# A one-core decoder layer: which queue writes the class-ordered attention values to DRAM, and when they are read back

## The chip, the cores and the metric

The kernel runs on one core of one Trainium2 chip. The metric is the device time of one execution in microseconds (us), the median over repeated runs. The engines are named as the profile names them: PE (TensorE, the matmuls), PEld (its weight loads), DVE (VectorE), ACT (ScalarE), POOL (GpSimd) and SP (SyncE). ACT, POOL and SP each issue DMAs from their own instruction stream, in program order: an instruction that waits holds up everything behind it on the same engine. PEq, ACTq, POOLq and SPq are the instruction queues of these engines.

## The reference

One layer of a decoder on x of 512 tokens by 1024 columns, float32. What matters here is the middle of it, the dilated attention; around it stand a gated linear attention, a merge, an MLP and a second gate:

```python
h = rmsnorm(x, ln1)
hq, hk, hv, hr, ha, hatt, hgate = split(h @ w_in)      # 9744 columns in all
o_gla = gla_mixer(hq, hk, hv, log_a)                    # gated linear attention, chunks of 64
hatt = hatt.reshape(B, S, 3 groups, 3 (q, k, v), 4 heads, 128)
for g, (win, dil) in enumerate(((128, 1), (512, 4), (2048, 16))):
    # a query sees keys t, t-dil, t-2*dil, ...: keys and values are gathered by stride
    o_g, lse_g = dilated_attention(q_g, k_g, v_g, bias_g, dil, win // dil)
wts = softmax(stack(lses), axis=0)                      # over the three groups
o_att = sum(wts * stack(outs))
mix = (sigmoid(g_gla) * (o_gla' @ w_o_gla) + sigmoid(g_att) * (o_att @ w_o_attn)) @ w_out
x = x + mix
x = x + relu(rmsnorm(x) @ w_mlp1)**2 @ w_mlp2
x = x + sigmoid(rmsnorm(x) @ w_pg) * (p @ w_pp)
return rmsnorm(x)
```

For the groups with stride 4 and 16 the kernel keeps the tokens ordered by class, token number modulo 4. Their values v1 and v2 (512 tokens by 512 columns each) leave the projection in natural order, so they are written to DRAM and read back with a stride of four rows: tile c of the result holds the tokens with t mod 4 = c.

## The kernel before

**The products.** All large products are done as one block level of a seven-product scheme (Strassen's, in Winograd's form), in float32 split into two parts `hi` and `lo`, with three matmuls for each pair. For each quarter of a weight matrix, called an operand, there are seven weight combinations, used in this order: A11, S1, A22, S2, A12, S4, S3. `strassen` (L338) runs them for most projections and `wide` (L384) for v1 and v2 together (the name is "v12"), as left-hand side 128 tokens by 512 columns. The projection after "v12" is "v0", the values of the first group, and the one after that "gq".

**How weights arrive.** `fetch` (L269) walks one list of operands, a few ahead of the matmul that needs them. For each it does four things, one operand apart: `prepare` (L238) issues the load on SP (L235), and, for the sum S1, a second load on POOL that adds to the tile in flight (L243); `sums` (L247) builds S2 and S4 on DVE (L255, L261) and, at S2, issues the accumulating load on POOL that turns the tile of A11 into S3 (L258); then ACT rounds `hi` (L281) and DVE subtracts `lo` (L276). There are six raw tiles `w`, five `hi` and four `lo`.

**The order of the work.** The program is written out in order by hand; nothing reorders it later but the hardware's own waits. Between pieces of eight or fewer matmuls `step` (L213) runs one entry of the list `later` (evacuations of PSUM and what follows them), and, after every so many matmul columns (`pace`), one step of a generator in `side` (work such as scores and softmax, up to the next `yield`); up to two generators in `side` take turns.

**The place of the change.** `values_cls` (L760) calls `wide`, whose `finish` is run from `later` once for each of the eight blocks of 128 tokens by 512 columns. `whole` (L740) makes the block: for six blocks a DVE add of PSUM to a partial sum (L422), for the last two an ACT copy out of PSUM (L744). POOL then writes the block to `v_dram` (L767). After the fourth block of a matrix, POOL reads the four tiles of that matrix back (L772). The last two blocks are finished during the first matmuls of "v0". Behind them on POOL come, in program order, the accumulating load L258 for operand S3 of "v0" and two small DMAs of the generator `weights` (L850): `k_dram` (L879) and `cc` (L880), which bring the softmax weights of the strided groups into natural order. `pv` (L890) uses `cc` first on DVE (L896), and the tiles v1 and v2 on PE (L932, L933), both during "gq".

Of the kernel before, what the change touches and what calls it, by code (L numbers as in the profile page):

```python
# [19 lines left out]
P = 128  # L20
# [161 lines left out]
def block_kernel(ctx, tc, xT, ws, pT, wts, wha, wa2, vec, lnf, rel, onehot, ident_d, mask_d, out):  # L182
    nc = tc.nc
    V, S, TE, SY, GP = nc.vector, nc.scalar, nc.tensor, nc.sync, nc.gpsimd
# [11 lines left out]
    def u32(name="u"):  # L196
        return ar.tile([P, T], F32, tag="u", name=name)
# [4 lines left out]
    def mmt():  # L202
        return mm.tile([P, T], F32, tag="mm", name="mmt")

    def smt():
        return sm.tile([P, T], F32, tag="sm", name="smt")


    side, later = [], []
# [78 lines left out]
    def weight(name, ahead=NW - 3):  # L288
        fetch(OPERAND[name] + ahead)
        return ready[name]  # L290

    def run(mms, n=PIECE, shared=False):
        for i in range(0, len(mms), n):
            for o, l, r, a, b in mms[i:i + n]:
                TE.matmul(o, lhsT=l, rhs=r, start=a, stop=b, skip_group_check=shared)  # L295
            step(n * r.shape[-1])
# [87 lines left out]
    def wide(name, xo, finish):  # L384


        bank, sums = {}, {}

        def begin(m, t, n, b):
            def go():  # L390
                sums[m, t, n] = u32()
                S.activation(sums[m, t, n], bank[b][n], AF.Copy, scale=-1.0 if m else 1.0)
            return go

        def end(m, t, n, b):
            return lambda: finish(m, t, n, sums.get((m, t, n)), bank[b][n])

        for i, (op, xname, b) in enumerate(WIDE):
            fresh = b not in bank
            if fresh:  # L400
                bank[b] = [smt() if b == "b" else mmt() for _ in range(2)]
            for pr in range(4):
                wh, wl = weight(f"{name}.{op}.{pr // 2}")
                xh, xl = xo(xname, pr)
                r = slice((pr % 2) * 512, (pr % 2 + 1) * 512)
                mms = []
                for n in range(2):
                    c = slice(n * P, (n + 1) * P)
                    for k, (l, w) in enumerate(((xh, wh), (xl, wh), (xh, wl))):
                        mms.append((bank[b][n], l[:, c], w[:, r], fresh and not pr and not k, pr == 3 and k == 2))  # L410
                run(mms, 3, shared=True)
            if i in WBEGIN:
                (m, t), b = WBEGIN[i]
                later[0:0] = [begin(m, t, n, b) for n in range(2)]
            if i in WEND:
                (m, t), b = WEND[i]
                later.extend(end(m, t, n, b) for n in range(2))
# [322 lines left out]
    def whole(m, s, ps):  # L740

        if s is None:
            s = u32()
            S.activation(s, ps, AF.Copy, scale=-1.0 if m else 1.0)  # L744
        else:
            add(m, s, s, ps)
        return s
# [12 lines left out]
    def values_cls(name):  # L760

        v_dram = [dr.tile([T, 512], F32, name=f"v{m}_dram") for m in range(2)]
        res, left = [[], []], [4, 4]

        def finish(m, t, n, s, ps):
            s, r = whole(m, s, ps), (2 * t + n) * P
            GP.dma_start(v_dram[m][r:r + P, :], s)  # L767
            left[m] -= 1
            if not left[m]:
                for c in range(4):  # L770
                    v = u32()
                    GP.dma_start(v, v_dram[m].rearrange("(m c) f -> c m f", c=4)[c])  # L772
                    res[m].append(v)

        wide(name, xs_op, finish)
        return res

    def softmax(ps, n0, bias, nm, sums, col, prob):
# [377 lines left out]
    side.append(scores12())  # L1156
    pace[0] = 3072
    v1, v2 = values_cls("v12")
    pace[0] = 2048
    side.append(weights())  # L1160
# [428 lines left out]
    def put(tt, c):  # L1589
        n = c.stop - c.start  # L1590
        o = u32()
        V.scalar_tensor_tensor(out=o[:, 0:n], in0=x2t[4 + tt][:, c], scalar=fr[:, tt:tt + 1], in1=lnb[1][:, c],
                               op0=OP.mult, op1=OP.mult)
        SY.dma_start(out[tt * P:(tt + 1) * P, 512 + c.start:512 + c.stop], o[:, 0:n])
# [112 lines left out]
```

## Time and profile before

| | |
|---|---|
| median time | 965.9 us |
| lowest time | 965.85 us |
| the profiled execution | 968.71 us |
| its span | 966.9 us |
| mean granted PE clock of the profiled execution | 0.994 |
| PE busy | 954.6 us, 99% |
| DVE busy | 740.6 us, 77% |
| ACT busy | 543.9 us, 56% |
| POOL busy | 101.5 us, 10% |
| moved by DMA | 140.97 MB, mean 146 GB/s |

The span runs from the first to the last instruction of the profiled execution; the execution's own time is 1.8 us longer. In a timeline row stand start and duration, engine, line, operation, output and inputs, how many, and in brackets how long the engine sat idle before it and what released it. A row of waits has the total, how often, and the longest. In a table by stretch come the length, busy time with the number of instructions for PE, PEld, DVE, ACT and POOL, then the granted PE clock (1.00 is full), the busy share of the 16 DMA engines and the GB/s that they moved.

### The profile page before, as it was taken

How to read it: one execution, taken by the hardware profiler on the slowest of the kernel's cores; microseconds unless marked ns; L12 is line 12 of the kernel's file. 1: busy time of each engine (PE TensorE's matmuls, PEld its weight loads, DVE VectorE, ACT ScalarE, POOL GpSimd, SP SyncE). 2: the span in 40 equal slices, each digit the busy share in tenths (PEclk: the TensorE clock that was granted, in tenths of full speed). 3: DMA queues.
4: the chain of work that ended last, by engine and by line, in shares of the span. 5: the costliest groups of instructions: out<-in, count | busy, mean ns of one | idle time of the engine just before them, and what ended most of it. 6: DMA issues, size and time to landing. Idle time of an engine off the chain costs nothing.

```text
span 966.9 us, 16069 instructions
## 1 busy us (share of the span) xinstructions
PE 954.6 (99%) x6398; PEld 880.4 (91%) x6398; DVE 740.6 (77%) x1062; ACT 543.9 (56%) x886; POOL 101.5 (10%) x143
## 2 busy tenths in 40 slices
PE   9999999989999999999999999999999999999997
PEld 8789998889998899999988889999998998998886
DVE  7698879746789669988765788777767999787754
ACT  7357547435575569776632346555655664354633
POOL 0140010220100012023001000010000000000000
PEclk9999999989999999999999999999999999999999
DMA  9374373965636554546526437556564374553102
GB/s 325 116 233 119 117 175 72 300 197 132 147 94 199 170 154 117 146 132 196 153 88 196 131 71 182 162 134 173 155 173 109 110 176 107 134 194 109 44 0 88
DMA packets 42923, 140.97 MB, mean 146 GB/s; under 512 B 6435, under 2 KB 7023, under 8 KB 42848
## 3 DMA queue, kind: packets, MB, share of 16 engines
q1 hardware_dynamic: 28224, 95.37, 29.3%
q0 software_dynamic: 12096, 42.17, 21.5%
q10 hardware_dynamic: 2528, 2.41, 0.7%
q8 instruction: 50, 0.82, 0.3%
q14 instruction: 25, 0.20, 0.1%
HBM read 133.60 MB, written 8.17 MB: 147 GB/s over the span
## 4 chain that ended last, share of the span: by engine, by line
PE 92%; DVE 3%; ACT 2%; DMA 1%; issue 1%; POOL 0%; POOLq 0%; DVEq 0%; ACTq 0%
PE mmt L295 77%; PE smt L295 6%; PE mmt L552 2%; PE smt L976 1%; DMA w<-in_wts_dram 1%; DVE lo L276 1%; PE smt L916 1%; PE smt L839 1%; DVE u L422 0%; PE smt L524 0%; ACT hi L281 0%; PE smt L933 0%; PE smt L809 0%; PE smt L932 0%; PE smt L922 0%
## 5 line engine op out<-in xcount | busy, mean ns | idle before, releaser
L295 PE MATMUL mmt<-ur,hi 128*128 128x256 f32 (+1 forms) x3120 | 635.8, 301 | 0.0
L295 PEld LDWEIGHTS mmt<-ur,hi 128*128 128x128 f32 x3120 | 500.7, 188 | 21.8
L295 PE MATMUL mmt<-ur,lo 128*128 128x256 f32 (+1 forms) x1560 | 470.7, 302 | 0.0
L276 DVE TENSOR_TENSOR lo<-w,hi 128x1024 fp32r<-128x1024 f32 x250 | 303.2, 1219 | 57.3 <-PE mmt L295 27.7
L281 ACT ACTIVATE hi<-w 128x1024 fp32r<-128x1024 f32 x250 | 260.9, 1054 | 110.6 <-PE mmt L295 25.9
L295 PEld LDWEIGHTS mmt<-ur,lo 128*128 128x128 f32 x1560 | 294.0, 188 | 10.9
L295 PE MATMUL mmt<-hi,ur 128*128 128x512 f32 (+3 forms) x480 | 134.7, 366 | 4.3 <-ACT u L369 4.3
L429 ACT ACTIVATE ur<-u 128x512 fp32r<-128x512 f32 x130 | 77.2, 624 | 98.1 <-DVE u L1241 30.8
L295 PEld LDWEIGHTS mmt<-hi,ur 128*128 128x128 f32 x480 | 87.0, 193 | 17.0 <-ACT u L369 4.5
L422 DVE TENSOR_TENSOR u<-u,mmt 128x512 f32<-128x512 f32 (+1 forms) x116 | 73.1, 655 | 38.1 <-PE mmt L295 37.9
L437 DVE TENSOR_TENSOR ur<-u,ur 128x512 fp32r<-128x512 f32 x129 | 84.8, 686 | 16.5 <-ACT ur L429 16.1
L295 PE MATMUL mmt<-lo,ur 128*128 128x512 f32 (+3 forms) x240 | 87.2, 363 | 0.0
L369 ACT ACTIVATE u<-mmt 128x512 f32<-128x512 f32 x88 | 52.3, 594 | 52.8 <-PE mmt L295 52.4
L243 POOL DMA_DIRECT2D w<-in_wts_dram x32 | 28.8, 923 | 309.6 <-DMA w<-in_wts_dram 102.8
L258 POOL DMA_DIRECT2D w<-in_wts_dram x24 | 21.2, 884 | 332.6 <-DVE w L255 239.8
L295 PEld LDWEIGHTS mmt<-lo,ur 128*128 128x128 f32 x240 | 46.3, 193 | 6.6
L295 PE MATMUL smt<-ur,hi 128*128 128x512 f32 x160 | 50.4, 393 | 0.1
L295 PEld LDWEIGHTS smt<-ur,hi 128*128 128x128 f32 x160 | 29.7, 188 | 8.1 <-PE smt L649 0.8
L295 PE MATMUL smt<-ur,lo 128*128 128x512 f32 x80 | 31.2, 390 | 0.0
L255 DVE TENSOR_TENSOR w<-w 128x1024 f32<-128x1024 f32 x24 | 29.4, 1225 | 0.8
L261 DVE TENSOR_TENSOR w<-w 128x1024 f32<-128x1024 f32 x24 | 29.4, 1225 | 0.8
L462 ACT ACTIVATE u<-u 128x512 f32<-128x512 f32 x24 | 14.9, 622 | 16.7 <-DVE u L1322 16.7
(213 smaller groups left out, 767.8 us busy)
## 6 DMA issues: line engine op xcount, KB each, us to landing
w<-in_wts_dram SPq DMA_DIRECT2D x170, 512.0 KB, 4.4
w<-in_wts_dram POOLq DMA_DIRECT2D x56, 512.0 KB, 5.7
u<-in_xT_dram SPq DMA_DIRECT2D x8, 256.0 KB, 5.0
u<-in_ws_dram SPq DMA_DIRECT2D x8, 256.0 KB, 5.2
v_dram<-u POOLq DMA_DIRECT2D x8, 256.0 KB, 9.1
u<-v_dram POOLq DMA_DIRECT2D x8, 256.0 KB, 6.1
y_dram<-u ACTq DMA_DIRECT2D x8, 256.0 KB, 3.6
u<-y_dram POOLq DMA_DIRECT2D x8, 256.0 KB, 5.9
```

What stands on the lines that cost most here:

```text
L243: GP.dma_start(w, wts[UNIT[b]], accum_op=OP.add)
L255: V.tensor_tensor(w, w, raw[f"{q}.A11"], op=OP.add)
L258: GP.dma_start(w, wts[UNIT[f"{q}.A21"]], accum_op=OP.add)
L261: V.tensor_tensor(w, w, raw[f"{q}.A12"], op=OP.add)
L276: V.tensor_tensor(lo, w, hi.bitcast(F32), op=OP.subtract)
L281: S.activation(hi, w, AF.Copy)
L295: TE.matmul(o, lhsT=l, rhs=r, start=a, stop=b, skip_group_check=shared)
L369: S.activation(sums[c], bank[b], AF.Copy, scale=-scale if c[0] else scale)
L422: V.tensor_tensor(out, s, ps, op=OP.subtract if m else OP.add)
L429: S.activation(hi, x, AF.Copy)
L437: V.tensor_tensor(lo, x, hi.bitcast(F32), op=OP.subtract)
L552: TE.matmul(q0ps[i], lhsT=(hi, hi, lo)[j][:, c], rhs=(xh, xl, xh)[j], start=not k and not j, stop=k == KC - 1 and j == 2)
```

## The change

The write of a block to `v_dram` is issued by ACT instead of POOL, and not in `finish` itself but in an entry that `finish` puts at the end of `later`, so some steps after the block is made. The read-back becomes a generator `back` in `side`. It waits, yielding, until all eight writes are issued, yields once more, and issues the four reads of the first matrix in one step and the four of the second in its next. The counter of writes left is one for both matrices.

```diff
     def values_cls(name):
 
         v_dram = [dr.tile([T, 512], F32, name=f"v{m}_dram") for m in range(2)]
-        res, left = [[], []], [4, 4]
+        res, left = [[], []], [8]
 
         def finish(m, t, n, s, ps):
             s, r = whole(m, s, ps), (2 * t + n) * P
-            GP.dma_start(v_dram[m][r:r + P, :], s)
-            left[m] -= 1
-            if not left[m]:
+
+            def put():
+                S.dma_start(v_dram[m][r:r + P, :], s)
+                left[0] -= 1
+            later.append(put)
+
+        def back():
+            while left[0]:
+                yield
+            yield
+            for m in range(2):
                 for c in range(4):
                     v = u32()
                     GP.dma_start(v, v_dram[m].rearrange("(m c) f -> c m f", c=4)[c])
                     res[m].append(v)
+                yield
 
         wide(name, xs_op, finish)
+        side.append(back())
         return res
```

The change adds ten lines, so lines of the kernel before from L773 on have numbers higher by ten in the kernel after; the write is L769 there and the read L780.

On POOL, from the last weight loads of "v12" to the first of "gk", before; `v_dram` is one of the two DRAM arrays, `u` a tile in SBUF:

```order
L243 DMA w<-in_wts_dram 128x1024 x5
L767 DMA v_dram<-u 128x512 x4
L243 DMA w<-in_wts_dram 128x1024
L767 DMA v_dram<-u 128x512 x2
L772 DMA u<-v_dram 128x512 x4
L258 DMA w<-in_wts_dram 128x1024
L767 DMA v_dram<-u 128x512 x2
L772 DMA u<-v_dram 128x512 x4
L879 DMA k_dram<-u 16x128
L880 DMA cc<-k_dram 128x4x4
L243 DMA w<-in_wts_dram 128x1024
L258 DMA w<-in_wts_dram 128x1024 x2
```

The same stretch on POOL after the change:

```order
L243 DMA w<-in_wts_dram 128x1024 x6
L258 DMA w<-in_wts_dram 128x1024
L780 DMA u<-v_dram 128x512 x8
L889 DMA k_dram<-u 16x128
L890 DMA cc<-k_dram 128x4x4
L243 DMA w<-in_wts_dram 128x1024
L258 DMA w<-in_wts_dram 128x1024 x2
```

The load for S3 of "v0" (the single L258) stood behind six writes and four reads and now has none of them ahead; all eight reads stand together behind it, and ahead of the two small DMAs.

On ACT, over the end of "v12" and the first operand of "v0", before; `e` with a number is a small tile of `weights`:

```order
L825 DMA u<-s_dram 32x128
L281 ACTIVATE hi<-w 128x1024 x8
L744 ACTIVATE u<-mmt 128x512
L861 ACTIVATE e_1987<-e_1987 128x16
L862 ACTIVATE e_1988<-e_1988 128x16
L744 ACTIVATE u<-mmt 128x512
L281 ACTIVATE hi<-w 128x1024
L369 ACTIVATE u<-mmt 128x512
```

The same stretch on ACT after the change:

```order
L835 DMA u<-s_dram 32x128
L281 ACTIVATE hi<-w 128x1024 x2
L769 DMA v_dram<-u 128x512 x2
L281 ACTIVATE hi<-w 128x1024 x2
L769 DMA v_dram<-u 128x512 x2
L281 ACTIVATE hi<-w 128x1024 x2
L769 DMA v_dram<-u 128x512 x2
L281 ACTIVATE hi<-w 128x1024 x2
L744 ACTIVATE u<-mmt 128x512 x2
L871 ACTIVATE e_1988<-e_1988 128x16
L872 ACTIVATE e_1989<-e_1989 128x16
L769 DMA v_dram<-u 128x512
```

Three pairs of writes now stand between the roundings of weights; of the last pair one stands here and the other behind the first evacuation of "v0" (L369), ahead of the rounding after it.

On DVE, over the same operands of "v0", before; `cn` and `dn` are small tiles of `weights`:

```order
L869 TENSOR_TENSOR cn_355<-e_1987,dn 128x16
L870 TENSOR_TENSOR cn_1991<-e_1988,dn 128x16
L276 TENSOR_TENSOR lo<-w,hi 128x1024
L261 TENSOR_TENSOR w<-w 128x1024
L877 COPY u<-smt 16x128
L276 TENSOR_TENSOR lo<-w,hi 128x1024 x4
```

And after:

```order
L879 TENSOR_TENSOR cn_355<-e_1988,dn 128x16
L880 TENSOR_TENSOR cn_1992<-e_1989,dn 128x16
L276 TENSOR_TENSOR lo<-w,hi 128x1024 x2
L887 COPY u<-smt 16x128
L276 TENSOR_TENSOR lo<-w,hi 128x1024 x2
```

Since `back` and `weights` take turns in `side`, the steps of `weights` come later: the copy that `k_dram` is written from now stands two operands further on, during the fifth operand of "v0" instead of the third.

## The prediction

> **What bounds the kernel now.** I start with the page's busy times and its chain, then ask which waits stopped PE.
>
> ```profile
> PE 954.6 (99%) x6398; PEld 880.4 (91%) x6398; DVE 740.6 (77%) x1062; ACT 543.9 (56%) x886; POOL 101.5 (10%) x143
> PE 92%; DVE 3%; ACT 2%; DMA 1%; issue 1%; POOL 0%; POOLq 0%; DVEq 0%; ACTq 0%
> ```
>
> PE is busy for 99% of the span and carries 92% of the chain. No change to DMA queues can therefore win more than what PE loses by waiting. The waits of PE over the whole span, most of all first:
>
> ```profile
> PE mmt L295 <- ACT u L369: 4.3, 1, 4.3
> PE smt L524 <- POOL ones L519: 1.0, 1, 1.0
> PE smt L976 <- DVE ur L1039: 0.2, 1, 0.2
> PE smt L916 <- ACT u L908: 0.2, 1, 0.2
> ```
>
> There is one wait of 4.3 us, one at the start that the change can't reach, and two of 0.2 us. The chain of the whole span shows where the long one lies and what is behind it:
>
> ```profile
> 194.86 11.38 DMA w<-in_wts_dram
> 207.87 0.94 ACT hi L281
> 209.35 8.62 PE mmt L295 x48
> ...
> 407.32 5.69 PE mmt L295 x48
> ```
>
> PE comes back at 209.35 us, and the chain before that is a weight load on its way for 11.38 us. ACT's rows name the load's customer, POOL's rows its issue:
>
> ```profile
> 206.32 1.06 ACT L281 ACTIVATE hi<-w 128x1024 fp32r<-128x1024 f32 x1 [11.98 <-DMA w<-in_wts_dram]
> 208.71 0.59 ACT L369 ACTIVATE u<-mmt 128x512 f32<-128x512 f32 x1
> 182.75 1.22 POOL L767 DMA_DIRECT2D v_dram<-u  x2 [0.72 <-DVE u L422]
> 192.75 2.13 POOL L772 DMA_DIRECT2D u<-v_dram  x4 [8.77 <-DMA v_dram<-u]
> 194.86 0.94 POOL L258 DMA_DIRECT2D w<-in_wts_dram  x1
> 195.42 1.48 POOL L767 DMA_DIRECT2D v_dram<-u  x2
> 208.43 2.14 POOL L772 DMA_DIRECT2D u<-v_dram  x4 [11.53 <-issue]
> 184.30 1.23 DVE L255 TENSOR_TENSOR w<-w 128x1024 f32<-128x1024 f32 x1
> ```
>
> ACT stood still for 11.98 us until operand S3 of "v0" had landed. POOL issued that load (L258) at 194.86. The data allowed it from 185.53 on, when DVE's L255 had read the raw tile (184.30 + 1.23). In between POOL sat for 8.77 us in front of the first read of `v_dram`, until the writes issued at 182.75 had landed, and then issued four reads. So POOL's program order made the load 194.86 - 185.53 = 9.3 us late. That the DMA engines were not the reason is in the stretches:
>
> ```profile
> 188.00:190.00 2.00, 2.00 (x19) 2.00 (x18) 1.90 (x7) 1.45 (x3) 0.00 (x0) 1.00 1.01 371
> 192.00:194.00 2.00, 2.00 (x19) 1.98 (x18) 1.21 (x2) 0.82 (x2) 1.25 (x3) 1.00 0.02 8
> 202.00:204.00 2.00, 2.00 (x20) 2.00 (x19) 0.00 (x0) 0.00 (x0) 0.00 (x0) 1.00 1.01 268
> 210.00:212.00 2.00, 2.00 (x11) 2.00 (x11) 1.97 (x4) 1.19 (x2) 1.07 (x3) 0.50 0.86 199
> ```
>
> Between 192 and 194 us the DMA engines are 2% busy while the load waits for its turn on POOL. By 202 us they are full again with the load, the reads and the writes together.
>
> **What the wait costs PE.** There are two terms. The idle time itself is in this row:
>
> ```profile
> 209.35 0.58 PE L295 MATMUL mmt<-hi,ur 128*128 128x256 f32 x1 [4.26 <-ACT u L369]
> ```
>
> The first term is 4.26 us. The second is the clock: the last stretch above has a granted clock of 0.50, and the 48 matmuls from 209.35 on take 8.62 us, while 48 of the same shape at 407.32 take 5.69. That is 2.93 us more. Together 7.19 us.
>
> **The change, part by part.**
>
> *The load for S3 goes ahead of the reads.* POOL's rows ahead of it are only weight loads now, so L258 is issued when L255 is done, at about 185.6. What does it take to land? The nearest rows are another accumulating load, issued just before on POOL, and the writes and reads of `v_dram` (the second row is of both):
>
> ```profile
> 181.12 0.91 POOL L243 DMA_DIRECT2D w<-in_wts_dram  x1 [2.36 <-DMA w<-in_wts_dram]
> DMA to landing us min/median/max: 9.2/9.2/9.3
> DMA to landing us min/median/max: 3.5/7.5/11.4
> ```
>
> The two accumulating loads between 160 and 190 us took 9.2 to 9.3 us; this one took 11.38 with reads and writes beside it. I take 9.3 and keep 11.4: landing at 194.9 to 197.0. From the start of the rounding to PE's start stand 209.35 - 206.32 = 3.03 us, and PE runs dry at 209.35 - 4.26 = 205.09, so a landing up to 202.0 costs nothing. The margin is 5 to 7 us, and both terms go: -7.2 us.
>
> *The writes move to ACT.* POOL loses eight issues, and ACT gets eight:
>
> ```profile
> L767 POOL DMA_DIRECT2D v_dram<-u x8: 539/555/941, 172.9 to 196.0; - x8
> L1180 ACTq DMA_DIRECT2D y_dram<-u x8: 326/326/344, 319.1 to 341.3; - x8
> y_dram<-u ACTq DMA_DIRECT2D x8, 256.0 KB, 3.6
> ```
>
> The kernel already writes blocks of this size from ACT, at 0.33 us each: 8 x 0.33 = 2.6 us of ACT's time, 0.65 us a pair. The wait that this adds matters more: a write waits for DVE's add, and the next roundings are queued behind it. The tightest pair:
>
> ```profile
> 176.65 1.28 DVE L422 TENSOR_TENSOR u<-u,mmt 128x512 f32<-128x512 f32 x2
> 176.80 1.06 ACT L281 ACTIVATE hi<-w 128x1024 fp32r<-128x1024 f32 x1 [0.85 <-PE mmt L295]
> 180.87 1.06 ACT L281 ACTIVATE hi<-w 128x1024 fp32r<-128x1024 f32 x1 [3.01 <-DMA w<-in_wts_dram]
> ```
>
> The adds end at 177.93, the two writes are issued by 178.3, and the rounding that stood at 176.80 starts 1.5 us later. The next one waits for a load until 180.87 anyway, so the delay ends there. The operand rounded at 176.80 is the first of "v0"; PE starts on it only behind the rest of "v12", so there is time. I cost the whole part at nothing. Without that cover it would be 1.5 us for this pair and at most the 2.6 us of issues.
>
> *The reads move behind the load, all eight together, and `weights` two operands back.* The rows that bound what comes late next:
>
> ```profile
> 190.76 0.60 ACT L369 ACTIVATE u<-mmt 128x512 f32<-128x512 f32 x1 [1.31 <-PE mmt L295]
> 210.55 0.52 POOL L879 DMA_DIRECT2D k_dram<-u  x1
> 216.75 0.79 POOL L880 DMA_DIRECT2D cc<-k_dram  x1 [5.68 <-DMA k_dram<-u]
> 217.54 0.92 POOL L243 DMA_DIRECT2D w<-in_wts_dram  x1
> 221.22 0.62 DVE L896 TENSOR_SCALAR u<-u,cc 128x256 f32<-128x256 f32 x2 [1.91 <-DMA cc<-k_dram]
> 223.34 0.44 PE smt L916 x4
> 234.45 0.22 PE smt L932 x2
> ```
>
> The last write is issued behind the evacuation at 190.76, so at about 191.4. It lands 3.5 to 11.4 later (the bounds above; I take the median, 7.5): 198.9, between 195 and 203. The last four reads take 2.1 to issue: 201.0, between 197 and 205. Then `k_dram` takes 216.75 - 210.55 = 6.2 until `cc` can be issued, and `cc` 221.22 - 216.75 = 4.5 until DVE goes on: 211.7, between 208 and 215.5. DVE wanted it at 221.22 - 1.91 = 219.31, and 7.2 earlier that is 212.1; PE wanted the result at 223.34, which is 1.5 after DVE's start, so PE tolerates `cc` until 223.34 - 0.62 - 7.2 = 215.5. The middle costs nothing and the far end just nothing; I take 0. The tiles v1 and v2 are used from 234.45 on, 227.2 after the shift; reads issued by 205 that take 11.4 land at 216.4. Copying the small tile for `k_dram` two operands later (2.85 us each at the 0.119 us a matmul of the 407.32 row, 5.7 in all) puts it near 198.5 instead of 192.8, still ahead of 201.0, when POOL can use it.
>
> *The weight loads behind.* POOL's next accumulating load, for "gk", stood behind `cc` at 217.5; now it comes at 201.0 + 6.2 + 0.8 = 208.0, which is 2.3 us sooner even against a PE that is 7.2 ahead.
>
> **The sum.** The removed wait is -4.26, the clock -2.93, the rest 0: -7.19. From 225 us on PE has hardly a wait (the 0.2 us rows), so the gain is carried to the end. The profiled execution would take 968.71 - 7.19 = 961.5 us. The runs' median is 965.9, which is 2.8 below that execution; I take the same difference from it: **958.7 us**, 0.7% faster.
>
> **Rivals.**
>
> *A shorter wait stays.* The load competes with the last writes while the DMA engines are full (1.01 at 188), and if it landed 2 to 5 us past 202.0, PE would wait that long. Against it: the longest landing in the rows, 11.4, ends at 197. A wait of 2 us gives 960.7, one of 4.26 with its clock loss gives 965.9; between them 960.7 to 964. The Trainium skill, "TensorE: Matmul & The Clock Gate", section "Part 1: The HAM clock gate", says that PE drops to half its clock after an idle window of about 3.4 us. The trace agrees on the half, with 0.50 after 4.26 us of idling; by that rule a remaining wait of 2 us would cost its own length only.
>
> *It only saves issue time.* If the DMA engines, and not POOL's order, set when S3 lands, moving the writes to another queue changes nothing for PE: POOL saves the issues that ACT spends, and the time is 965.9. For it speaks the share of 1.01 while the load is under way; against it the share of 0.02 at 192 to 194, with the load unissued. The Trainium skill, "DMA: Bandwidth & Descriptors", section "Issuing engines are not separate DMA queues", states this: all issuers share the same 16 engines, and issuing from several saves only the sequencer's time. By that rule the gain on POOL would be 8 x 0.55 = 4.4 us of an engine that is 10% busy. What the rule leaves out, and POOL's rows show, is the wait in program order.
>
> *`cc` comes too late, and the change loses.* The eight reads wait for all eight writes, and two small DMAs that depend on each other come after them. If both, among reads that fill the engines, took 11.4 instead of 6.2 and 4.5, behind writes that land at 203, then `cc` would land at 205 + 22.8 = 227.8, 12.3 past what PE tolerates. With 2.9 for the clock that is +15.2 - 7.2 = +8.0: 973.9. It decides against the change from a landing of about 215.5 + 4.3 = 219.8 on, since 4.3 us of waiting with 2.9 of clock undo the gain. Against it: both small DMAs took 6.2 and 4.5 in a stretch with a DMA share of 0.86.
>
> **How the numbers follow.** The chances: the wait goes and nothing takes its place, 957.5 to 960.5: 0.72. A shorter wait stays, 960.5 to 965: 0.12. Only issue time, 965 to 967: 0.06. `cc` too late, 966 to 974: 0.05. More is won than I see, since POOL's later loads also come sooner, 955 to 957: 0.05. The likeliest gives the time. A range from 956.5 to 964.0 holds the first case, three quarters of the second and a part of the last, 0.72 + 0.09 + 0.02 = 0.83, with the spread between runs in it. All cases lie within 2% of 965.9 (946.6 to 985.2), about what a measurement of this kernel can tell from no change; I leave 0.02 on each side for what I haven't seen.
>
> **What would show it.** Right: the wait of 4.3 us for L369 is gone from PE's list and the granted clock is 1.00 between 205 and 216; the load of S3 is issued at 185 to 187 with POOL waiting for DVE's L255 ahead of it; ACT's idle time ahead of the rounding of S3 is 1 to 3 us instead of 12; PE ends 7 us earlier, and the stretch from 225 to the end is as long as before. Wrong: a new PE wait at 205 (the load is slow), at 212 to 220 (`cc`), or at 178 to 193 (ACT held by the writes). The step I am least sure of is how long the last writes take to land from ACT, since `cc` hangs on it.

## The result, and the profile after

The kernel after takes 960.62 us in the median (960.23 to 960.88 over six runs), the kernel before 967.38 beside it: ratio 0.9931, 95% interval 0.9917 to 0.9946, so 0.5 to 0.8% faster. The profiled execution of the kernel after took 960.88 us with a span of 959.1 us; of the kernel before it was 968.71 and 966.9. One of the six runs of the kernel before took 2431.07 us and does not count in the ratio; the 965.9 us that the prediction started from was the median of the first three of them, that run included. The prediction had 958.7, with a range from 956.5 to 964.0.

The busy times and the chain of the kernel after:

```profile
PE 951.2 (99%) x6398; PEld 877.5 (91%) x6398; DVE 740.4 (77%) x1062; ACT 544.1 (57%) x886; POOL 97.3 (10%) x135
PE 94%; DVE 3%; ACT 1%; issue 1%; POOL 0%; POOLq 0%; DVEq 0%; ACTq 0%
```

The same 6398 matmuls are busy for 3.4 us less, most of it the clock, and the weight load has gone from the chain. The waits of PE over the whole span, all of them:

```profile
PE smt L524 <- POOL ones L519: 1.0, 1, 1.0
PE smt L986 <- DVE ur L1049: 0.2, 1, 0.2
```

The wait of 4.3 us for L369 is gone, and the 0.2 us at the transposes too. POOL's rows of the kernel after, with the load for S3 second:

```profile
181.31 0.88 POOL L243 DMA_DIRECT2D w<-in_wts_dram  x1 [9.15 <-DMA w<-in_wts_dram]
185.70 0.87 POOL L258 DMA_DIRECT2D w<-in_wts_dram  x1 [3.51 <-DVE w L255]
195.17 2.19 POOL L780 DMA_DIRECT2D u<-v_dram  x4 [8.60 <-DMA v_dram<-u]
197.91 2.13 POOL L780 DMA_DIRECT2D u<-v_dram  x4 [0.56 <-DMA w<-in_wts_dram]
200.46 0.52 POOL L889 DMA_DIRECT2D k_dram<-u  x1 [0.42 <-DVE lo L276]
208.59 0.80 POOL L890 DMA_DIRECT2D cc<-k_dram  x1 [7.61 <-DMA k_dram<-u]
```

The load is issued at 185.70 instead of 194.86, released by DVE's L255. The wait of 8.6 us for the landing of the writes is still there, but now it stands behind the load. What ACT and DVE make of it:

```profile
178.04 1.06 ACT L281 ACTIVATE hi<-w 128x1024 fp32r<-128x1024 f32 x1 [2.31 <-DVE u L422]
183.83 1.06 ACT L281 ACTIVATE hi<-w 128x1024 fp32r<-128x1024 f32 x1 [1.56 <-DMA v_dram<-u]
195.19 1.06 ACT L281 ACTIVATE hi<-w 128x1024 fp32r<-128x1024 f32 x1 [1.31 <-DMA w<-in_wts_dram]
211.97 0.61 DVE L906 TENSOR_SCALAR u<-u,cc 128x256 f32<-128x256 f32 x2
```

ACT rounds S3 at 195.19 instead of 206.32, after 1.31 us of waiting instead of 11.98. DVE doesn't wait for `cc` at all, where it had waited 1.91 us. The two rows above those are ACT's new waits. The stretches at the place of the old wait:

```profile
204.00:206.00 2.00, 2.00 (x19) 2.00 (x18) 1.65 (x2) 0.83 (x1) 0.00 (x0) 1.00 0.97 379
212.00:216.00 4.00, 4.00 (x37) 4.00 (x35) 3.97 (x10) 1.43 (x2) 0.00 (x0) 1.00 0.92 226
```

PE runs through at a granted clock of 1.00, in the stretches between these two as well.

### The profile page after: what moved, and what is told of

It is laid out like the page before. It is cut to its first block, busy times and chain, and to the rows that moved or that the text cites. A ratio compares the mean times of both kernels' runs of the same rounds, so it can differ in the third digit from the quotient of the medians.

```text
span 959.1 us, 16066 instructions
## 1 busy us (share of the span) xinstructions
PE 951.2 (99%) x6398; PEld 877.5 (91%) x6398; DVE 740.4 (77%) x1062; ACT 544.1 (57%) x886; POOL 97.3 (10%) x135
## 4 chain that ended last, share of the span: by engine, by line
PE 94%; DVE 3%; ACT 1%; issue 1%; POOL 0%; POOLq 0%; DVEq 0%; ACTq 0%
PE mmt L295 78%; PE smt L295 6%; PE mmt L552 2%; PE smt L986 1%; DVE lo L276 1%; PE smt L926 1%; PE smt L849 1%; DVE u L422 0%; PE smt L524 0%; PE smt L819 0%; PE smt L943 0%; PE smt L942 0%; PE smt L932 0%; PE smt L818 0%; PE smt L1550 0%
## 5 line engine op out<-in xcount | busy, mean ns | idle before, releaser
L295 PE MATMUL mmt<-hi,ur 128*128 128x512 f32 (+3 forms) x480 | 132.4, 361 | 0.0
L369 ACT ACTIVATE u<-mmt 128x512 f32<-128x512 f32 x88 | 52.2, 594 | 54.5 <-PE mmt L295 54.2
L258 POOL DMA_DIRECT2D w<-in_wts_dram x24 | 21.3, 890 | 335.6 <-DVE w L255 222.1
L255 DVE TENSOR_TENSOR w<-w 128x1024 f32<-128x1024 f32 x24 | 29.4, 1225 | 0.8
```

The source lines that it names most:

```text
L255: V.tensor_tensor(w, w, raw[f"{q}.A11"], op=OP.add)
L258: GP.dma_start(w, wts[UNIT[f"{q}.A21"]], accum_op=OP.add)
L369: S.activation(sums[c], bank[b], AF.Copy, scale=-scale if c[0] else scale)
```

## The experiments

**Two halves of the change.** The change does two things at once, and the theory (POOL's program order held the load back) needs only one of them. The first half alone puts the writes on ACT and leaves the reads ahead of the load:

```diff
 (kernel before, finish)
-            GP.dma_start(v_dram[m][r:r + P, :], s)
-            left[m] -= 1
-            if not left[m]:
-                ...the four reads
+            def put():
+                S.dma_start(v_dram[m][r:r + P, :], s)
+                left[m] -= 1
+                if not left[m]:
+                    ...the four reads
+            later.append(put)
```

> One half of the change alone: the writes go to ACT as in the kernel after, the four reads of a matrix stay where they were, on POOL right behind its fourth write, so four reads still stand ahead of the load for S3 of v0. Theory (POOL's program order): the reads wait until the writes issued at about 183 us have landed, the load is issued at about 194 to 195 us as before, PE waits 3.5 to 5 us at 205 us with the clock at half behind it; 966 to 968 us, ratio to before 0.998 to 1.002. Rival (what counts is that the writes leave POOL's queue for ACT's): PE has no wait, ratio 0.993.

Measured: 964.82 us beside 965.21 of the kernel before, ratio 1.0004 (0.9988 to 1.0020). The ratios come from the single runs, so they can differ a little from the quotient of the two medians. This one is as expected; the time is below the expected 966 to 968, since the kernel before was at 965.21 in this set and not at 967.38. Waits of PE, POOL's rows and ACT's rounding of S3 in this kernel:

```profile
PE mmt L295 <- ACT u L369: 4.7, 1, 4.7
193.24 2.18 POOL L774 DMA_DIRECT2D u<-v_dram  x4 [10.76 <-DMA v_dram<-u]
195.40 0.96 POOL L258 DMA_DIRECT2D w<-in_wts_dram  x1
206.17 1.06 ACT L281 ACTIVATE hi<-w 128x1024 fp32r<-128x1024 f32 x1 [12.46 <-DMA w<-in_wts_dram]
```

At the load nothing has changed: POOL waits 10.76 us for the landing, the load goes out at 195.40, PE waits 4.7 us. Moving the writes to another queue alone is worth nothing that these runs can tell: the interval leaves at most 0.12% of gain. The Trainium skill, "DMA: Bandwidth & Descriptors", section "Issuing engines are not separate DMA queues", says that another issuer saves only issue time; this run agrees with it, with its ratio of 1.0004.

The second half alone leaves the writes on POOL and makes only the reads side work:

```diff
 (kernel after, finish)
-            def put():
-                S.dma_start(v_dram[m][r:r + P, :], s)
-                left[0] -= 1
-            later.append(put)
+            GP.dma_start(v_dram[m][r:r + P, :], s)
+            left[0] -= 1
```

> The other half alone: the writes stay on POOL, in finish, and only the reads become side work behind the load for S3. Theory (POOL's program order): the writes ahead of the load wait only for DVE's adds, which end at 183 us, so the load is issued at 185.5 to 186 us and lands by 197; no PE wait at 205; ratio 0.992 to 0.995, the whole gain. Rival (the writes must leave POOL): the load still comes at 190 us or later and a wait of 2 to 4 us stays, ratio 0.996 to 1.000.

Measured: 960.40 us, ratio 0.9955 (0.9939 to 0.9970). POOL's rows:

```profile
185.24 0.90 POOL L258 DMA_DIRECT2D w<-in_wts_dram  x1 [2.12 <-DVE w L255]
187.25 1.22 POOL L767 DMA_DIRECT2D v_dram<-u  x2 [1.11 <-ACT u L744]
191.86 2.13 POOL L777 DMA_DIRECT2D u<-v_dram  x4 [3.39 <-DMA v_dram<-u]
```

The load is issued at 185.24, a little ahead of the expected 185.5 to 186, and PE has no wait at 205. The time is that of the whole change (960.40 and 960.62). The ratio is nearer to one than the expected 0.992 to 0.995 because the kernel before ran at 965.21 here and at 967.38 beside the kernel after; more on that below. So the whole gain is in the place of the reads.

**The wait, or the traffic.** Four reads ahead of the load do two things: they make POOL wait, and they put a megabyte on the DMA engines beside the load. In this kernel the order on POOL is that of the kernel before, but the reads of the first matrix take an input that is there from the start, and the values of that matrix are left out:

```diff
 (kernel before, finish)
-                    GP.dma_start(v, v_dram[m].rearrange("(m c) f -> c m f", c=4)[c])
+                    GP.dma_start(v, v_dram[m].rearrange("(m c) f -> c m f", c=4)[c] if m else
+                                 xT.rearrange("(m c) f -> c m f", c=8)[c])
```

> The kernel before with its order on POOL unchanged, but the four reads of the first matrix take rows of the input x (same size, 2 KB a partition) instead of what was just written, so they have nothing to wait for; the values of that matrix are left out by this. Theory (the cost is the wait in POOL's order, not the reads' traffic): the four reads are issued at 184 to 186 us, the load at 186 to 187, landing 9 to 12 later, by 199; no PE wait at 205; ratio 0.992 to 0.995. Rival (the load lands late because the reads fill the DMA engines beside it): it lands past 202 although issued early, PE waits 1 to 4 us, ratio 0.995 to 1.000.

Measured: 960.44 us, ratio 0.9956 (0.9943 to 0.9969). POOL's rows and the rounding of S3:

```profile
183.08 2.14 POOL L772 DMA_DIRECT2D u<-in_xT_dram  x4
185.92 0.90 POOL L258 DMA_DIRECT2D w<-in_wts_dram  x1 [0.70 <-DVE nmx L859]
196.41 1.06 ACT L281 ACTIVATE hi<-w 128x1024 fp32r<-128x1024 f32 x1 [2.95 <-DMA w<-in_wts_dram]
```

The reads go out at once, the load at 185.92, and it is there at 196.4 although the reads run beside it: 10.4 us to land, against 9.5 in the kernel after. Without the wait the traffic costs PE nothing. The ratio misses the expected 0.992 to 0.995 for the same reason as with the reads alone: the time is that of the kernel after.

**How much room there is.** In the next four kernels POOL is kept busy ahead of the load of the kernel after, by memsets of a constant tile to the value that it has:

```diff
 (kernel after, sums)
+            if q == "v0":
+                for _ in range(32):        # 50, 60, 72
+                    GP.memset(ones, 1.0)
             GP.dma_start(w, wts[UNIT[f"{q}.A21"]], accum_op=OP.add)
```

> The kernel after with 32 small memsets of a constant tile on POOL ahead of the load for S3, each waiting for the one before, 0.2 to 0.35 us each: the load is issued at 188.6 to 193.4 us instead of 185.7 and lands 9.5 later, 198 to 203. Theory (PE needs the load landed by 202, so there is a margin of some 6 us): no PE wait, or one under 1 us; 960 to 962 us. Rival (there is no margin, each us of delay is a us of time): 3 to 8 us more than the kernel after, 964 to 968.

> The kernel after with 50 memsets of 0.27 us on POOL ahead of the load for S3 of v0 (32 of them moved its issue to 190.8 us): issue at about 195.3, landing 6 to 11 later, 201 to 206. Theory (PE needs it landed by 202 and each us past that costs one; a short wait leaves the clock alone): PE waits 0 to 4 us, the time is that of the kernel after (960.6) plus the wait, 960.6 to 964.6, with the clock at 1.00 behind a wait under 3 us. Rival (any wait costs the clock too): 2.9 us more than the wait.

> The same with 60 memsets: issue at about 198.0, landing 204 to 209. Theory: PE waits 2 to 7 us; from about 4 us on 2.9 us for the clock come on top; 962.6 to 970.5. In the profile the sum must hold: span of the kernel after + wait + what the matmuls behind it take longer. Rival (something else than PE's wait for this load made the kernel before slower): the time stays near 961 although the wait is there, or moves without it.

> The same with 72 memsets: issue at about 201.3, landing 207 to 212. Theory: PE waits 5 to 10 us, with the clock at 0.5 for about 6 us behind it (2.9 us); 968.5 to 973.5. Rival (the clock loss grows with the wait): more than 3.5 us of it.

These kernels were run in two later sets, in which the kernel before had medians of 965.21 (with the 32 memsets) and 965.07 us; the kernel after was not run again in them, so its 960.62 is compared across sets. In the table, the last row is the first profile of the kernel before, with the median of the first set. "Rounded" is the start of ACT's rounding of S3, "wait" PE's wait for L369, "way" the time from the first matmul of "v0" to the first transpose of `pv`, all from the profiled execution, "rest" is the way less 23.05 us (the kernel after) less all waits of PE in it: what the matmuls took longer.

| kernel | load issued | rounded | wait | way | rest | median time |
|---|---|---|---|---|---|---|
| after | 185.70 | 195.19 | 0 | 23.05 | 0 | 960.62 |
| 32 memsets | 190.84 | 196.54 | 0 | 23.02 | 0 | 960.90 |
| 50 memsets | 195.08 | 201.86 | 0.64 | 25.00 | 0.4 | 962.08 |
| 60 memsets | 197.34 | 202.55 | 1.28 | 25.63 | 0.4 | 963.75 |
| 72 memsets | 200.98 | 206.40 | 5.10 | 30.28 | 2.1 | 967.62 |
| before | 194.86 | 206.32 | 4.26 | 30.12 | 2.8 | 967.38 |

With 32 memsets the load is issued 5.1 us later, lands 1.4 us later, and costs nothing that the runs can tell (960.90 and 960.62). With 50 the rounding starts at 201.86 and PE waits 0.64 us; this execution's "v0" started 0.9 us earlier than that of the kernel before (186.79 and 187.69), so the limit of 202.0 holds to within 0.2 us. With 50 and 60 there is a second wait of 0.94 us just ahead of the transposes, for DVE, which had itself stood still for 5.99 and 6.62 us until ACT had rounded S3. With 72 memsets the kernel after is as slow as the kernel before (ratio 1.0018, 1.0003 to 1.0033), by the same wait, and PE's list has no other new one. The waits of PE and the stretch behind, with 60 memsets and then with 72:

```profile
PE mmt L298 <- ACT u L372: 1.3, 1, 1.3
PE smt L929 <- DVE u L909: 0.9, 1, 0.9
206.00:208.00 2.00, 2.00 (x19) 2.00 (x18) 2.00 (x3) 1.42 (x2) 0.00 (x0) 1.00 0.96 369
```

```profile
PE mmt L298 <- ACT u L372: 5.1, 1, 5.1
210.00:212.00 2.00, 2.00 (x12) 2.00 (x11) 1.97 (x4) 1.26 (x2) 0.00 (x0) 0.50 0.99 387
```

Waits of 1.3 and 0.9 us left the clock at 1.00; behind the wait of 5.1 us it is 0.50. Some expectations missed. The load landed sooner than forecast with 32 memsets (196.5, not 198 to 203), with 60 (202.6, not 204 to 209) and with 72 (206.4, not 207 to 212); so with 60 PE waited 1.3 us and not 2 to 7. With 72 the time was 967.6 and not 968.5 to 973.5, because the clock cost 2.1 us instead of 2.9.

**The rival on the other side: `cc` too late.** Here POOL is kept busy between the write of `k_dram` and the read of `cc`:

```diff
 (kernel after, weights)
+        for _ in range(55):
+            GP.memset(ones, 1.0)
         GP.dma_start(cc, k_dram.rearrange("h (m c) -> m h c", c=4))
```

> The kernel after with 55 memsets on POOL between the write of k_dram and the read of cc, 14.9 us where POOL waited 7.6 us anyway: cc is issued at about 215.9 instead of 208.6 us and lands 2.4 to 4.5 later, 218.3 to 220.4. Theory (PE tolerates cc until about 215.5): PE waits 2.5 to 5.5 us for the transposes behind it, and the clock adds up to 2.9; 963 to 969. Rival (cc has far more room than that, since PE has other work): 960.6 to 961.5.

Measured: 964.08 us, ratio 0.9987 (0.9976 to 0.9998). DVE's first use of `cc`, and PE's wait behind it:

```profile
216.29 0.67 DVE L908 TENSOR_SCALAR u<-u,cc 128x256 f32<-128x256 f32 x2 [4.60 <-DMA cc<-k_dram]
PE smt L928 <- DVE u L908: 2.7, 2, 1.3
```

`cc` was issued at 213.97 instead of 208.59 and DVE went on at 216.29, both some 2 us ahead of what was expected (215.9, and 218.3 to 220.4). PE waited 2.7 us, twice 1.34, and the time rose by 3.5 us, with the clock at 1.00 throughout. That the 2.7 us lie in the expected 2.5 to 5.5 is luck: the first wait alone is half of it, and the second, which was not forecast, made up for the early landing. 216.29 less the first 1.34 is 214.95, and this execution's "v0" started 1.0 us before that of the kernel before (186.71), so PE tolerates `cc` until 215.9 in its time, where the forecast had 215.5. The mechanism of this rival is real; the change stays more than 3 us short of it, since DVE had `cc` by 211.97.

**Why the kernel before is unsteady.** Its times in all the sets, the one named above aside, spread over 962.8 to 969.5 us, while those of the kernel after lie within 0.7 us. Three more profiles of the kernel before:

> The kernel before once more, for another profile: its executions have spread from 962.8 to 969.5 us while those of the kernel after lie within 0.7. Theory (the wait for S3 and the clock behind it differ from execution to execution, and the first profile was one of the long ones): the time less 960.6 is this execution's PE wait at 205 us plus what the 48 matmuls behind it take over 5.69 us, to within 1 us; in a short execution the load lands earlier or the clock stays. Rival (the spread comes from elsewhere in the kernel): wait and clock loss are 4.3 and 2.9 again whatever the time.

> As for the first repetition of the kernel before: the time less 960.6 equals PE wait plus clock loss of this execution, to within 1 us; the rival has 4.3 + 2.9 whatever the time.

> As for the first repetition of the kernel before: the time less 960.6 equals PE wait plus clock loss of this execution, to within 1 us; the rival has 4.3 + 2.9 whatever the time.

| execution | time | wait at 205 | way | rest |
|---|---|---|---|---|
| first profile | 968.71 | 4.26 | 30.12 | 2.8 |
| again 1 | 965.27 | 1.91 | 26.64 | 1.7 |
| again 2 | 968.02 | 4.58 | 30.10 | 2.5 |
| again 3 | 966.27 | 3.42 | 28.11 | 1.6 |

The way alone explains 7.1, 3.6, 7.1 and 5.1 us over the kernel after; the times are 8.1, 4.7, 7.4 and 5.7 over 960.6. What is left, 0.4 to 1.1 us, I did not follow up in full; up to 0.4 of it are small waits at the transposes. So wait and clock explain two of the four to within the 1 us that was set, and miss it by less than 0.1 in the other two. The wait differs because the load's landing does (9.9 to 11.7 us in these four), and the clock loss does not follow the wait. The shortest one in PE's row and the stretches behind it:

```profile
206.60 0.51 PE L295 MATMUL mmt<-hi,ur 128*128 128x256 f32 x2 [1.91 <-ACT u L369]
206.00:208.00 2.00, 1.40 (x10) 1.40 (x11) 1.90 (x3) 2.00 (x4) 0.57 (x2) 0.94 0.55 102
208.00:210.00 2.00, 2.00 (x11) 2.00 (x11) 1.97 (x2) 0.44 (x1) 2.00 (x4) 0.50 0.73 227
210.00:212.00 2.00, 2.00 (x14) 2.00 (x14) 1.68 (x4) 1.57 (x2) 0.07 (x1) 0.70 0.91 260
```

The 0.94 and 0.70 are means: in stretches of 0.2 us the granted clock of these profiles is 1.00 or 0.50, with a value between only where it changes. So each profile with a wait of 1.9 us or more has one time at half clock around it, and its ends can be read. In the table, "half of PE's run in it" is half of the part of that time in which PE was at work.

| profile | PE goes on | half clock from | to | length | half of PE's run in it | rest |
|---|---|---|---|---|---|---|
| before, first | 209.35 | 208.54 | 215.37 | 6.83 | 3.0 | 2.8 |
| before, again 1 | 206.60 | 207.77 | 211.18 | 3.41 | 1.7 | 1.7 |
| before, again 2 | 209.03 | 207.11 | 213.93 | 6.82 | 2.5 | 2.5 |
| before, again 3 | 208.41 | 208.28 | 211.69 | 3.41 | 1.6 | 1.6 |
| writes on ACT alone | 209.20 | 207.40 | 214.22 | 6.82 | 2.5 | 2.4 |
| 72 memsets | 209.42 | 206.88 | 213.70 | 6.82 | 2.1 | 2.1 |

The half clock lasts 3.41 us or twice that, and what it costs is half of what PE runs in it, to within 0.2 us of the rest; the part that falls into the wait costs nothing. Its start is not tied to the wait's end: it comes 2.5 us ahead of it with 72 memsets and 1.2 us behind it in "again 1". In the 3.41 us ahead of each start PE had been idle for 1.91 us or more, while the waits of 1.28 and 1.34 us above brought no half clock. In its first 3.41 us PE was idle for at most 0.13 us in the two short ones and for 0.81 us or more in the long ones. That these idle shares decide is an inference from six profiles; no run was made to test it.

## Why the prediction was right, point by point

**What bounds the kernel, and the one wait.** Right. The PE wait at 205 us was the only thing to win, and it was won whole: the way from the first matmul of "v0" to the transposes fell from 30.12 to 23.05 us, 7.07, where the two terms had 7.19. From the transposes to the last evacuation the kernel before takes 735.7 us and the kernel after 735.4, so the gain was carried to the end.

**The load for S3.** Right: issued at 185.70 (forecast 185.6), landed by 195.2 (194.9 to 197.0), with the limit at 202.0 borne out by the delayed kernels. That POOL's order and not the DMA engines' load was the cause is shown by the reads that had nothing to wait for.

**The writes on ACT.** The cost was nothing, as forecast, but not all of the waits were: the rounding at 178.04 (176.80 before) waited for DVE's adds, as worked out, and the one at 183.83 stood 1.56 us for the landing of an earlier write (by its row), which I had not seen. Both ended in waits that were there before. And the half of the change that this is brings no gain of its own, as the run with it alone shows; in the sum it stood with 0.

**The reads and `cc`.** The last write was issued at 190.4 (forecast 191.4), the last four reads were out by 200.0 (201.0), `cc` was issued at 208.59 (207.2), and DVE used it at 211.97 without a wait (211.7 against a want at 212.1). `k_dram` took longer than in the row that I used, 8.1 us until `cc` could go instead of 6.2, and `cc` itself less. The two misses cancel.

**The time.** This is the step that was mis-sized: "I take the same difference from it". I took the 2.8 us by which the profiled execution lay above the median for an offset that would stay. It was not one: the profiled execution of the kernel after lies 0.26 above its median. The difference was for the most part the wait and the clock loss themselves, as the four profiles of the kernel before show, and this profile had caught one of the longer executions. The sum made on the profiled execution, 961.5, was within 0.9 us of the 960.6 measured; with the offset taken off again it became 958.7, 1.9 too low. A part of the miss lies in the 965.9 itself, the median of only three runs: the five runs that count in the ratio have a median of 967.30, and 7.19 below that is 960.1. For the same reason the gain in percent depends on which runs of the kernel before stand beside it: 0.69% there, 0.45% with the reads alone, at the same time of the faster kernel. And the 2% that the prediction took for what a measurement of this kernel can tell was too much: six runs told 0.7% within 0.15% either way.

**The rivals.** "It only saves issue time" has fallen for the change as a whole; for its first half the run agrees with it, within its interval. "`cc` comes too late" would work as described, more than 3 us further on. In "a shorter wait stays" I let a rule on the clock give a wait of 2 us its own length only. The runs say otherwise: an execution with a wait of 1.91 us ran at half its clock behind it and lost 1.7 us more, while waits of 1.3 and 0.9 us left the clock alone. The Trainium skill, "TensorE: Matmul & The Clock Gate", section "Part 1: The HAM clock gate", has the idle window at about 3.4 us and calls it free-running; the halved clock, its length of once or twice 3.41 us and its start at different points of the wait or behind it agree with that, the 1.91 us does not, since PE was not idle for a whole window there.

## What to carry to other kernels

An engine that issues DMAs in program order should not have a DMA that must wait for another's landing ahead of one that something urgent needs: look for a DMA issue with a long wait in the issuing engine's rows, and see what stands behind it. Moving the dependent DMA back behind the urgent one was worth the whole gain here, moving its predecessor to another queue nothing that could be told. And when a profile's execution lies above the median, ask first whether the very wait that you mean to remove is the reason; then the sum is made on that execution and not shifted.

## What the runs showed of the hardware that I had not expected

- The clock loss behind a wait is not a fixed price: 1.6 to 2.8 us behind waits of 1.91 to 5.10 us, and not in their order (1.7 behind 1.91, 1.6 behind 3.42, 2.1 behind 5.10). The half clock lasts 3.41 or 6.83 us, and the loss is half of what PE runs in it. What sets the moment at which it begins stays open.
- The writes of 256 KB from ACT took as long to land as from POOL in this stretch, 8.9 us in the median against 9.1, though the same kind of write takes 3.6 us later in the kernel; the DMA engines' share was 1.02 to 1.06 here, in the kernel after from 172 to 194 us.
- The same accumulating load took 5.2 to 11.7 us to land: 9.9 to 11.7 with four reads issued just ahead of it (10.4 where they read x), 9.5 in the kernel after, and 5.2 to 6.8 in the kernels that issue it 5 to 15 us later.
